# Output-projection weights rounded behind the latest attention work on ScalarE and GpSimd, and the second layer's modulation behind the last softmax denominators

## The chip, the core and the metric

The kernel runs on one core of a Trainium2 chip. The core has a matrix engine (PE, whose weight loads are listed apart as PEld), a vector engine (DVE), a scalar engine (ACT), GpSimd (POOL), and SyncE (SP), from whose queue all transfers here are issued. Each engine works through its own list of instructions in order. The metric is the time of one execution in microseconds (us), the median of several runs.

## What is computed

The reference is a two-layer diffusion backbone in float32 over 2048 latent and 256 context tokens of width 1024. Layer 0 has two attention mixers side by side, a windowed one (8 heads) and a latent-compressed one ("mixer B", 8 heads of 64, over all 2304 keys). Layer 1 has neighbourhood attention (16 heads). Each layer ends in a gated output projection; scale, shift and gate of the next layer come from the conditioning vectors.

```
# mixer B (layer 0): every latent query reads all keys
s = (einsum('bqhd,bkhd->bhqk', qn, kn) + einsum('bqhr,bkr->bhqk', qr, kr)) * scale
p = softmax(s);  ob = einsum('bhqk,bkhd->bqhd', p, v)
# output projection of layer 0, gated
y = concatenate([oa * silu(za), ob * silu(zb)]) @ out_w
# modulation of a layer: one linear map of silu(c), of silu(c_ctx) for context rows
mod = silu(c) @ ada_w + ada_b
```

## The kernel before

Stages run in this order: in0 (input projection), attn_a (windowed attention), out_open(0), attn_b (mixer B), outp(0) (output projection of layer 0), in1, out_open(1), attn_c (neighbourhood attention), outp(1). Most products are three PE matmuls on a rounded high part and a remainder: high x high, low x high, high x low. A matrix that comes from HBM is therefore *split* first: `wsplit` lets ACT copy the loaded tile ws into a rounded tile wh (L260) and POOL subtract it from ws to give the remainder wl (L261). For the output-projection weights these tiles are called wso, who and wlo.

A scheduler lays out the instructions of each engine. It may move an instruction ahead of others that were written before it, where its model of the program lets it start earlier; in attn_b only PE's order is the written one. `tc.issue_after(x)` forbids it to place the instructions inside ahead of instruction x on x's engine.

**attn_b** goes through 8 heads of 2304 queries, in units of 512 queries: t0 = 0, 512, 1024, 1536 and one short unit of 256 for the context. A unit has 18 key tiles. For each tile PE makes three score matmuls (L977 to L979) into one of three PSUM buffers `bs`, ACT takes the exponential twice, rounded into `bph` (L982) and full in place (L983), DVE makes the remainder `bpl` (L984), POOL adds `bph` to the running row sum `bacc` (L988), and four tiles later PE multiplies both parts with the values (`bo`, L997 and L998). `bph` and `bpl` have 8 buffers each. The next tile's L977 into a `bs` buffer needs the L984 that last read it. Between these PE computes the row maxima of the next unit (`bm`, L941, reduced by DVE, L943). At the end of a unit ACT, DVE and POOL take the output out (L1002 to L1007) and PE transposes the row sum (`bdt`, L1015), from which DVE (L1017) makes the denominators.

The weights of the output projection are prepared during the attention. `out_weights_apart` returns, for each of 7 row blocks k of 128 (in layer 1: 3), a step load(k), two transfers on SP, and a step split(k), two `who` on ACT and two `wlo` on POOL. The load buffers wst hold 3 tiles. attn_b runs one such step at units 512 and 1536 of each head from the second: load(k) in the first of them, split(k) in the second. Both stand under an issue_after on the head's value transfer. The eighth block is split by outp itself. attn_c runs them from its 17th item on, at every second one.

**outp(0)**: for each of 8 row blocks the gated input G is made from transfers `o` or `oo` (output), `oz` (gate) and `ord` (one over the denominators, by way of the HBM array s_rd): DVE L1144 to L1146, ACT L1148, POOL L1149 (Gg, Gkh, Gkl). PE makes `y` (L1183). The last denominators of attn_b go through `den_piece`: DVE L675 reciprocal, PE L677 transpose `dnb`, DVE L679 copy `dnsb`, SP L680 store to s_rd. From its third work item on, outp(0) runs four steps (OSIDE) of `mod_rows` for each item, the modulation of layer 1: transfers scb (L190) and adat (L198), ACT L191, and DVE products `mj` (L200).

Of the kernel before, what the change touches and what calls it, by code (L numbers as in the profile page):

```python
# [100 lines left out]
class Kern:  # L101
# [570 lines left out]
    def den_piece(self, p, pt, den, n, dst, nm, tag="pt"):  # L672

        nc = self.nc
        nc.vector.reciprocal(den[:, :n], den[:, :n])  # L675
        ps = pt.tile([P, 512], F32, tag=tag, name=f"dn{nm}")
        nc.tensor.transpose(ps[:n, 0:P], den[:, :n], self.ident)  # L677
        s = p.tile([P, P], F32, tag="dns", bufs=2, name=f"dns{nm}")
        nc.vector.tensor_copy(s[:n, :], ps[:n, 0:P])  # L679
        nc.sync.dma_start(dst.rearrange("(t q) -> t q", q=P), s[:n, :])  # L680
# [169 lines left out]
    def out_weights_apart(self, l, k0, k1, rings):  # L850

        st = {}

        def load(k):
            st[k] = [self.wload(self.wop, self.i[f"wo{l}"][k * P : (k + 1) * P, hf * 512 : (hf + 1) * 512],
                                512, f"o{l}{k}{hf}") for hf in range(2)]

        def split(k):
            self.W.append([self.wsplit(rings, s, 512, f"o{l}{k}{hf}") for hf, s in enumerate(st.pop(k))])
        return [x for k in range(k0, k1) for x in (lambda k=k: load(k), lambda k=k: split(k))]  # L860

    def attn_b(self):
# [5 lines left out]
        with ExitStack() as ctx:  # L868
# [96 lines left out]
            def st_pieces(h, t0, n):  # L965
                t = H[h]
                c = t0 // P
                kts = list(range(NT)) if t0 < TL else [NTL, NTL + 1]
                st = {}

                def score(j):
                    kt = kts[j]
                    if j == 0:
                        st["acc"] = p1.tile([P, 512], F32, tag="acc", bufs=3, name=f"bacc{h}_{c}")
                    ps = sp.tile([P, 512], F32, tag="s", name=f"bs{h}_{c}_{j}")
                    ks, qs = slice(kt * P, (kt + 1) * P), slice(t0, t0 + n)
                    nc.tensor.matmul(ps[:, :n], t["kh"][0:97, ks], t["qh"][0:97, qs], start=True, stop=False)  # L977
                    nc.tensor.matmul(ps[:, :n], t["kh"][0:96, ks], t["ql"][0:96, qs], start=False, stop=False)  # L978
                    nc.tensor.matmul(ps[:, :n], t["kl"][0:96, ks], t["qh"][0:96, qs], start=False, stop=True)  # L979
                    hi = ph.tile([P, 512], R32, name=f"bph{h}_{c}_{j}")  # L980
                    lo = pl_.tile([P, 512], R32, name=f"bpl{h}_{c}_{j}")
                    nc.scalar.activation(hi[:, :n], ps[:, :n], AF.Exp)  # L982
                    nc.scalar.activation(ps[:, :n], ps[:, :n], AF.Exp)  # L983
                    nc.vector.tensor_sub(lo[:, :n], ps[:, :n], f(hi[:, :n]))  # L984
                    if j == 0:
                        st["h0"] = hi
                    else:
                        nc.gpsimd.tensor_add(st["acc"][:, :n], f((st["h0"] if j == 1 else st["acc"])[:, :n]), f(hi[:, :n]))  # L988
                    st[j] = (hi, lo)

                def pv(j):
                    if j == 0:
                        st["o"] = op.tile([P, 512], F32, tag="o", name=f"bo{h}_{c}")
                        st["o2"] = op.tile([P, 512], F32, tag="o2", name=f"bo2{h}_{c}")
                    hi, lo = st.pop(j)
                    fi, la = j == 0, j == len(kts) - 1
                    nc.tensor.matmul(st["o"][:, :n], t["v"][:, kts[j], 0:P], hi[:, :n], start=fi, stop=la)  # L997
                    nc.tensor.matmul(st["o2"][0:65, :n], t["v"][:, kts[j], 64 : P + 1], lo[:, :n], start=fi, stop=la)  # L998

                def fin():  # L1000
                    o = p.tile([P, 512], F32, tag="os", name=f"bos{h}_{c}")
                    nc.scalar.activation(o[:, :n], st["o"][:, :n], AF.Copy)  # L1002
                    o2 = p.tile([65, 512], F32, tag="os2", name=f"bos2{h}_{c}")
                    nc.vector.tensor_copy(o2[:, :n], st["o2"][0:65, :n])
                    acc = st["acc"]
                    nc.gpsimd.tensor_add(o[0:64, :n], o2[0:64, :n], o[0:64, :n])
                    nc.gpsimd.tensor_add(acc[64:65, :n], o2[64:65, :n], acc[64:65, :n])  # L1007
                    for e in range(2):
                        nc.sync.dma_start(scr["o0"][e, 512 + h * 64 : 576 + h * 64, t0 : t0 + n], o[e * 64 : e * 64 + 64, :n])

                def den():
                    d, c0 = den_of(h, t0)
                    ps = xp.tile([P, 512], F32, tag="x", name=f"bdt{h}_{c}")
                    for x in range(n // P):
                        nc.tensor.transpose(ps[:, x * P : (x + 1) * P], st["acc"][:, x * P : (x + 1) * P], self.ident)  # L1015
                    col = t0 // P - c0
                    nc.vector.tensor_reduce(d[:, col : col + n // P], ps[:, :n].rearrange("p (t k) -> p t k", k=P), AX.X, ALU.add)  # L1017
                    late.put(8, lambda: den_done(h, t0, n))

                k = range(len(kts))  # L1020
                return [lambda j=j: score(j) for j in k], [lambda j=j: pv(j) for j in k], fin, den
# [53 lines left out]
    def outp(self, l):  # L1075
        nc, tc, i, scr = self.nc, self.tc, self.i, self.scr
        with ExitStack() as ctx:
# [108 lines left out]
            for n, (c, tt) in enumerate(work):  # L1186
                if tt == 0 and c + 1 < len(chunks):
                    gs = gsteps(c + 1)
                if n + 2 < len(work):
                    c2, t2 = work[n + 2]  # L1190
                    X[(c2, t2)] = res(chunks[c2][0] + t2 * P, c2, t2)
                a = chunks[c][0] + tt * P
                if n < 3:

                    if n == 0:
                        Y = [ytile(x) for x in range(3)]
                        for k in range(KB):
                            for x in range(3):
                                product(Y[x], 0, x, k)
                    ps = Y[n]  # L1200
                else:
                    ps = ytile(n)
                    for k in range(KB):
                        product(ps, c, tt, k)
                x = X[(c, tt)]
                gv = gate[:, 1 if a >= TL else 0, :]
                y = p.tile([P, D], F32, tag="ry", bufs=2, name=f"ry{l}{n}")
                nc.vector.tensor_tensor(y, ps, gv, ALU.mult)
                nc.vector.tensor_add(y, y, x)
                if l == 0:  # L1210
                    lt.put(1, lambda a=a, y=y: nc.sync.dma_start(scr["h1"][a : a + P, :], y))
                else:
                    junk = p.tile([P, D], BF16, tag="oj", bufs=1, name=f"oj{n}")
                    ss = p.tile([P, 1], F32, tag="oss", bufs=3, name=f"oss{n}")
                    nc.scalar.activation(junk, y, AF.Square, accum_out=ss)
                    r = self.rstd(p, ss, D, "o")
                    nc.vector.scalar_tensor_tensor(y, y, r, fg, ALU.mult, ALU.mult)
                    lt.put(1, lambda a=a, y=y: nc.sync.dma_start(self.out[a : a + P, :], y))
                lt.tick()
                for _ in range(OSIDE):  # L1220
                    if side and n > 1:
                        side.pop(0)()
                left = max(1, chunks[c][1] // P - 1 - tt)
                for _ in range(-(-len(gs) // left)):
                    if gs:
                        gs.pop(0)()
# [144 lines left out]
    def attn_c(self):  # L1371
# [5 lines left out]
        with ExitStack() as ctx:  # L1377
# [63 lines left out]
            def make_bias(h, cb):  # L1441
                if cb == 2:
                    return
                b = bias[nbias[0] % 2]
                nbias[0] += 1
                bu = H[h][3]

                for rt, u0, w, d0 in ((0, 128, 384, 128), (1, 0, 512, 0), (2, 0, 384, 128)):
                    nc.gpsimd.tensor_add(b[:, rt, d0 : d0 + w], bu[:, CT[cb], u0 : u0 + w], rm[:, rt, 512 - w : 512])  # L1449
                cur[(h, CT[cb])] = b  # L1450

            def s_pieces(h, cb):
# [7 lines left out]
                def go(rg):  # L1460
# [18 lines left out]
                        op0=ALU.add, op1=ALU.min, accum_out=nm)  # L1479
                    d, c0 = den_of(h, cb)  # L1480
                    col = cb * 4 + rg - c0
                    nc.scalar.activation(s[:, :n], s[:, :n], AF.Exp, bias=nm, scale=-1.0,  # L1482
                                         accum_out=d[:, col : col + 1])
                    Pt[rg] = s
                return [lambda rg=rg: go(rg) for rg in range(4)], Pt

# [193 lines left out]
```

## Time and profile before

| | |
|---|---|
| median of 3 runs | 3673.56 us (3673.25 to 3679.89) |
| the profiled execution | 3666.66 us, of which the span of its instructions is 3664.8 us |
| granted TensorE clock, mean | 0.978 |
| attn_b | about 962 to 1915 us of the span |
| outp(0) | to about 2143 us |
| in1 | to about 2877 us |
| attn_c | about 2877 to 3460 us |

The trace is one execution on the chip. Times in the rows are microseconds from the start of the span. "PE bs L977 <- DVE bpl L984" means that PE stood still before its instruction of line 977 until DVE's of line 984 had ended. PEclk is the share of TensorE's full clock that was granted: 1.00 is the higher of its two levels (2.4 GHz), 0.50 the lower one (1.2 GHz).

### The profile page before, as it was taken

What the parts mean: (1) busy time and instruction counts of PE and PEld (TensorE: products, weight loads), DVE (VectorE), ACT (ScalarE), POOL (GpSimd) and SP (SyncE); (2) the same over time, 40 slices, a digit from 0 to 9 for tenths busy, and PEclk for the clock granted to TensorE, in tenths of its full rate; (3) what the DMA queues carried; (4) which work ended last, traced back from release to release, by engine and by line L of the source; (5) the groups of instructions that cost most, each with busy time, mean ns of one, the idle gap of its engine ahead of it and who ended that gap; (6) DMA issues with size and microseconds to landing.
All of it is one profiled execution on the core that took longest, in us unless ns stands there. A gap on an engine that the chain in (4) does not pass through costs nothing. (4 is left out here: it accounts for less than half of the span.)

```text
span 3664.8 us, 52981 instructions
## 1 busy us (share of the span) xinstructions
PE 3474.2 (95%) x17607; PEld 2871.1 (78%) x17607; DVE 2293.3 (63%) x4313; ACT 1904.1 (52%) x3808; POOL 1759.3 (48%) x1655
## 2 busy tenths in 40 slices
PE   6999989999999999998999999999999999999888
PEld 5787778899877777776767878888888799999766
DVE  6445542399988888987988872213111088888565
ACT  4344333399777777766761142223221288888511
POOL 6555553211488888988893252224122143333432
PEclk8999999999999999999999999999999999999999
DMA  6768564763320222123039955554445476666685
GB/s 218 219 199 261 171 184 128 227 173 83 82 60 18 68 68 68 24 54 80 23 115 302 292 183 168 167 144 127 130 140 146 158 287 238 233 228 231 192 234 172
DMA packets 381051, 576.76 MB, mean 157 GB/s; under 512 B 35393, under 2 KB 218081, under 8 KB 370913
## 3 DMA queue, kind: packets, MB, share of 16 engines
q1 hardware_dynamic: 380777, 573.39, 51.3%
q8 instruction: 138, 2.26, 0.3%
q14 instruction: 136, 1.11, 0.1%
HBM read 399.36 MB, written 173.90 MB: 156 GB/s over the span
## 5 line engine op out<-in xcount | busy, mean ns | idle before, releaser
L261 POOL TENSOR_TENSOR wl<-ws,wh 128x512 fp32r<-128x512 f32 (+2 forms) x320 | 427.1, 1351 | 642.6 <-ACT wh L260 579.2
L988 POOL TENSOR_TENSOR bacc<-bacc,bph 128x512 f32<-128x512 f32 (+1 forms) x528 | 667.5, 1267 | 33.5 <-ACT bph L982 1.8
L982 ACT ACTIVATE bph<-bs 128x512 fp32r<-128x512 f32 (+1 forms) x610 | 353.3, 579 | 215.2 <-PE bs L979 188.8
L943 DVE TENSOR_REDUCE bmx<-bm 128x1 f32<-128x512 f32 (+1 forms) x656 | 406.6, 628 | 67.5 <-PE bm L941 51.5
L984 DVE TENSOR_TENSOR bpl<-bs,bph 128x512 fp32r<-128x512 f32 (+1 forms) x610 | 401.3, 659 | 59.4 <-ACT bs L983 58.1
L983 ACT ACTIVATE bs<-bs 128x512 f32<-128x512 f32 (+1 forms) x610 | 350.7, 575 | 0.0
L260 ACT ACTIVATE wh<-ws 128x512 fp32r<-128x512 f32 (+2 forms) x328 | 197.1, 613 | 266.6 <-DMA ws<-in_w_dram 211.2
L267 PE MATMUL mm<-Uh,wh 128*128 128x512 f32 (+1 forms) x832 | 325.2, 391 | 0.0
L268 PE MATMUL mm<-Ul,wh 128*128 128x512 f32 (+1 forms) x832 | 323.8, 389 | 0.0
L269 PE MATMUL mm<-Uh,wl 128*128 128x512 f32 (+1 forms) x832 | 322.0, 390 | 0.4 <-DVE wl L261 0.4
L1449 POOL TENSOR_TENSOR cbias<-cbu,rm 128x384 f32<-128x384 f32 x144 | 158.3, 1113 | 333.9 <-DVE cnm L1477 194.4
L1477 DVE CUSTOM_DVE_ANT_0 cp<-cs,cbias 128x640 f32<-128x640 f32 (+1 forms) x256 | 222.3, 886 | 135.7 <-PE cs L1473 91.1
L977 PE MATMUL bs<-bqh,bkh 97*128 97x512 f32 (+1 forms) x610 | 246.6, 404 | 42.9 <-DVE bpl L984 42.2
L997 PE MATMUL bo<-bph,bv 128*128 128x512 f32 (+1 forms) x610 | 242.3, 397 | 15.4 <-ACT bos L1002 15.2
L941 PE MATMUL bm<-bkh,bqh 96*128 96x512 f32 (+1 forms) x656 | 244.3, 387 | 4.5 <-DVE bmx L943 3.6
L240 DVE TENSOR_TENSOR plc<-ptc,phc 128x512 fp32r<-128x512 f32 (+1 forms) x384 | 235.3, 640 | 18.1 <-ACT phc L239 17.3
L978 PE MATMUL bs<-bql,bkh 96*128 96x512 f32 (+1 forms) x610 | 240.7, 395 | 0.0
L979 PE MATMUL bs<-bqh,bkl 96*128 96x512 f32 (+1 forms) x610 | 239.0, 392 | 0.0
L998 PE MATMUL bo<-bpl,bv 128*65 128x512 f32 (+1 forms) x610 | 238.0, 390 | 0.4 <-DVE bpl L984 0.2
L200 DVE SCALAR_TENSOR_TENSOR mj<-adat,scb 128x512 bf16<-128x512 f32 x144 | 121.9, 847 | 185.7 <-DMA adat<-in_adat_dram 165.6
L1482 ACT ACTIVATE cp<-cp,cnm 128x640 f32<-128x640 f32 (+1 forms) x256 | 226.3, 884 | 17.6 <-DVE cnm L1477 17.4
L239 ACT ACTIVATE phc<-ptc 128x512 fp32r<-128x512 f32 (+1 forms) x384 | 205.4, 560 | 55.1 <-PE ptc L647 50.8
(314 smaller groups left out, 8870.6 us busy)
## 6 DMA issues: line engine op xcount, KB each, us to landing
ws<-in_w_dram SPq DMA_DIRECT2D x256, 256.0 KB
ck<-s_kcT SPq DMA_DIRECT2D x32, 1152.0 KB
cv<-s_vc SPq DMA_DIRECT2D x64, 512.0 KB
adat<-in_adat_dram SPq DMA_DIRECT2D x96, 256.0 KB
o<-s_o SPq DMA_DIRECT2D x40, 512.0 KB
s_z<-zs SPq DMA_DIRECT2D x64, 256.0 KB
s_qcT<-st SPq DMA_DIRECT2D x64, 256.0 KB
s_kcT<-st SPq DMA_DIRECT2D x32, 512.0 KB
```

The source lines that it names most:

```text
L261: (eng or nc.gpsimd).tensor_sub(l[:, :w], s[:, :w], f(h[:, :w]))
L267: nc.tensor.matmul(out, a[0], b[0], start=first, stop=False)
L268: nc.tensor.matmul(out, a[0], b[1], start=False, stop=False)
L269: nc.tensor.matmul(out, a[1], b[0], start=False, stop=last)
L941: nc.tensor.matmul(ps[:, :w], t["qh"][0:96, b * P : (b + 1) * P], t["kh"][0:96, k0 : k0 + w], start=True, stop=True)
L943: nc.vector.tensor_reduce(t["mx"][:, j : j + 1], ps[:, :w], AX.X, ALU.max)
L977: nc.tensor.matmul(ps[:, :n], t["kh"][0:97, ks], t["qh"][0:97, qs], start=True, stop=False)
L982: nc.scalar.activation(hi[:, :n], ps[:, :n], AF.Exp)
L983: nc.scalar.activation(ps[:, :n], ps[:, :n], AF.Exp)
L984: nc.vector.tensor_sub(lo[:, :n], ps[:, :n], f(hi[:, :n]))
L988: nc.gpsimd.tensor_add(st["acc"][:, :n], f((st["h0"] if j == 1 else st["acc"])[:, :n]), f(hi[:, :n]))
L997: nc.tensor.matmul(st["o"][:, :n], t["v"][:, kts[j], 0:P], hi[:, :n], start=fi, stop=la)
```

## The change

The attention now keeps its latest instruction in two fields: `self.acts` on ACT (the full exponential of a tile in attn_b, of a row group in attn_c) and `self.pools` on POOL (an addition to the row sum in attn_b, of the bias in attn_c). split(k) stands under issue_after of both. `den_piece` keeps its reciprocal in `self.recip`, and the modulation's steps in outp(0) stand under issue_after of that. No instruction is added or removed.

```diff
     def den_piece(...):
-        nc.vector.reciprocal(den[:, :n], den[:, :n])
+        self.recip = nc.vector.reciprocal(den[:, :n], den[:, :n]).ins
...
         def split(k):
-            self.W.append([self.wsplit(...) for hf, s in enumerate(st.pop(k))])
+            with self.tc.issue_after(self.acts), self.tc.issue_after(self.pools):
+                self.W.append([self.wsplit(...) for hf, s in enumerate(st.pop(k))])
...
     def attn_b(self):
-                    nc.scalar.activation(ps[:, :n], ps[:, :n], AF.Exp)
+                    self.acts = nc.scalar.activation(ps[:, :n], ps[:, :n], AF.Exp).ins
...
-                        nc.gpsimd.tensor_add(st["acc"]...)
+                        self.pools = nc.gpsimd.tensor_add(st["acc"]...).ins
...
     def outp(self, l):
                 for _ in range(OSIDE):
                     if side and n > 1:
-                        side.pop(0)()
+                        with tc.issue_after(self.recip):
+                            side.pop(0)()
...
     def attn_c(self):
-                    nc.gpsimd.tensor_add(b[:, rt, d0 : d0 + w], ...)
+                    self.pools = nc.gpsimd.tensor_add(b[:, rt, d0 : d0 + w], ...).ins
...
-                    nc.scalar.activation(s[:, :n], s[:, :n], AF.Exp, bias=nm, ...)
+                    self.acts = nc.scalar.activation(s[:, :n], s[:, :n], AF.Exp, bias=nm, ...).ins
```

The lines of the changed kernel stand one to five further down than those of the kernel before. In names such as bph1_8_17 the numbers are head, first query tile of the unit, and key tile; the last number only tells instances apart.

ACT in head 1, around the first split. Before, it stands behind tile 8 of the head's first unit:

```order
L982 ACTIVATE bph1_0_8_12314<-bs1_0_8_12310 128x512
L983 ACTIVATE bs1_0_8_12310<-bs1_0_8_12310 128x512
L260 ACTIVATE who000_13123<-wso000_12503 128x512
L260 ACTIVATE who001_13127<-wso001_12505 128x512
L982 ACTIVATE bph1_0_9_12336<-bs1_0_9_12332 128x512
L983 ACTIVATE bs1_0_9_12332<-bs1_0_9_12332 128x512
```

and now:

```order
L984 ACTIVATE bph1_8_17_13111<-bs1_8_17_13107 128x512
L985 ACTIVATE bs1_8_17_13107<-bs1_8_17_13107 128x512
L260 ACTIVATE who000_13123<-wso000_12503 128x512
L260 ACTIVATE who001_13127<-wso001_12505 128x512
L984 ACTIVATE bph1_12_0_13136<-bs1_12_0_13132 128x512
L985 ACTIVATE bs1_12_0_13132<-bs1_12_0_13132 128x512
```

The pair has moved from tile 8 of unit 0 to the start of unit 1536, 95 rows further on; heads 2 to 6 show the same.

POOL in head 7, in its last long unit (tile 12 on), while the first G (Gkl) of outp(0) is already being made. Before:

```order
L1006 TENSOR_TENSOR bos7_8_21015<-bos27_8_21017,bos7_8_21015 64x512
L988 TENSOR_TENSOR bacc7_8_20670<-bacc7_8_20670,bph7_8_17_20945 128x512
L988 TENSOR_TENSOR bacc7_12_20961<-bacc7_12_20961,bph7_12_3_21007 128x512
L1149 TENSOR_TENSOR Gkl00_21267<-o005_21330,Gql00_21265 128x512
L1007 TENSOR_TENSOR bacc7_8_20670<-bos27_8_21017,bacc7_8_20670 1x512
L988 TENSOR_TENSOR bacc7_12_20961<-bacc7_12_20961,bph7_12_4_21027 128x512
```

and now:

```order
L990 TENSOR_TENSOR bacc7_12_20961<-bacc7_12_20961,bph7_12_3_21007 128x512
L990 TENSOR_TENSOR bacc7_8_20670<-bacc7_8_20670,bph7_8_17_20945 128x512
L261 TENSOR_TENSOR wlo060_20954<-wso060_20353,who060_20953 128x512
L261 TENSOR_TENSOR wlo061_20958<-wso061_20355,who061_20957 128x512
L990 TENSOR_TENSOR bacc7_12_20961<-bacc7_12_20961,bph7_12_4_21027 128x512
L1010 TENSOR_TENSOR bacc7_8_20670<-bos27_8_21017,bacc7_8_20670 1x512
L1152 TENSOR_TENSOR Gkl00_21267<-o005_21330,Gql00_21265 128x512
```

The seventh split, which stood in head 6, is now here, and the Gkl of row block 5 has four more instructions ahead of it.

DVE at the start of outp(0), around the last denominators (denb). Before:

```order
L1146 TENSOR_TENSOR oo012_21543<-oo012_21543,oz012_21544 128x512
L200 SCALAR_TENSOR_TENSOR mj1_000_21610,mcol0_21607<-adat1_0_0_21608,scb0_21603 128x512
L200 SCALAR_TENSOR_TENSOR mj1_010_21612,mcol0_21607<-adat1_0_0_21608,scb0_21603 128x512
L200 SCALAR_TENSOR_TENSOR mj1_100_21616,mcol0_21607<-adat1_1_0_21614,scb0_21603 128x512
L200 SCALAR_TENSOR_TENSOR mj1_110_21618,mcol0_21607<-adat1_1_0_21614,scb0_21603 128x512
L1017 TENSOR_REDUCE denb7_1536_21222<-bdt7_12_21223 128x4
```

and now:

```order
L1149 TENSOR_TENSOR oo012_21543<-oo012_21543,oz012_21544 128x512
L1020 TENSOR_REDUCE denb7_1536_21222<-bdt7_12_21223 128x4
L675 RECIPROCAL denb7_1536_21222<-denb7_1536_21222 128x4
L200 SCALAR_TENSOR_TENSOR mj1_000_21610,mcol0_21607<-adat1_0_0_21608,scb0_21603 128x512
L200 SCALAR_TENSOR_TENSOR mj1_010_21612,mcol0_21607<-adat1_0_0_21608,scb0_21603 128x512
```

The denominators' reduction and reciprocal have passed the modulation's products.

## Rows read from the trace of the kernel before

**Rows 1.** The page's first part: busy time, share, instructions of each engine.

```profile
PE 3474.2 (95%) x17607; PEld 2871.1 (78%) x17607; DVE 2293.3 (63%) x4313; ACT 1904.1 (52%) x3808; POOL 1759.3 (48%) x1655
```

**Rows 2.** PE's waits, 950 to 1970 us: total us, times, longest us.

```profile
PE bs L977 <- DVE bpl L984: 42.2, 14, 6.9
PE bo L997 <- ACT bos L1002: 15.2, 38, 0.8
PE dnb L677 <- DVE denb L675: 8.3, 1, 8.3
```

**Rows 3.** Waits of the other engines in the same stretch.

```profile
ACT who L260 <- DMA wso<-in_wo_dram: 43.3, 6, 8.1
POOL wlo L261 <- ACT who L260: 37.7, 5, 9.4
ACT bph L982 <- POOL bacc L988: 19.8, 30, 2.6
```

**Rows 4.** SP's order of time, head 1: start, us, queue, line, transfer, count.

```profile
1086.81 9.88 SPq L254 DMA_DIRECT2D wso<-in_wo_dram  x2
```

**Rows 5.** ACT's order of time there; in brackets the idle time before.

```profile
1093.49 0.59 ACT L983 ACTIVATE bs<-bs 128x512 f32<-128x512 f32 x1
1102.18 1.29 ACT L260 ACTIVATE who<-wso 128x512 fp32r<-128x512 f32 x2 [8.10 <-DMA wso<-in_wo_dram]
```

**Rows 6.** PE's order of time there.

```profile
1105.23 0.79 PE L977 MATMUL bs<-bqh,bkh 97*128 97x512 f32 x1 [6.91 <-DVE bpl L984]
```

**Rows 7.** Stretches: length, busy us (count) of PE, PEld, DVE, ACT, POOL, then PEclk.

```profile
1105.20:1109.40 4.20, 4.17 (x10) 3.20 (x11) 3.90 (x7) 2.34 (x5) 3.96 (x4) 0.50 0.00 0
1109.40:1113.60 4.20, 4.20 (x22) 3.35 (x21) 2.81 (x7) 3.63 (x7) 3.96 (x4) 0.99 0.00 0
```

**Rows 8.** Stretches, tile 9 of unit 0 to unit 512: six heads (first, last, sum), head 7.

```profile
1093.80:1116.00 22.20, 15.29 (x62) 11.53 (x62) 12.23 (x24) 10.94 (x21) 13.98 (x12) 0.85 0.39 101
...
1685.90:1708.70 22.80, 16.51 (x63) 12.53 (x63) 12.16 (x24) 11.96 (x23) 15.15 (x13) 0.78 0.55 146
...
sum 131.80, PE 95.83 PEld 72.39 DVE 73.23 ACT 67.02 POOL 85.12; mean PE 15.97 PEld 12.06 DVE 12.21 ACT 11.17 POOL 14.19
...
1810.90:1824.20 13.30, 13.30 (x64) 10.32 (x63) 12.32 (x25) 10.07 (x19) 12.52 (x11) 1.00 0.00 1
```

**Rows 9.** Stretches, unit 512 of head 5 and of head 6.

```profile
1589.30:1616.10 26.80, 26.44 (x119) 20.34 (x118) 24.37 (x45) 20.29 (x39) 23.30 (x19) 1.00 0.05 11
1708.70:1741.20 32.50, 29.75 (x120) 22.02 (x119) 25.04 (x45) 20.63 (x39) 28.43 (x23) 0.89 0.04 9
```

**Rows 10.** Stretch of head 1 without a stall, to the next head's split.

```profile
1109.40:1217.00 107.60, 105.62 (x481) 81.28 (x479) 96.01 (x179) 79.73 (x150) 94.39 (x76) 1.00 0.23 50
```

**Rows 11.** ACT in head 6, unit 512: the longest wait for a bph buffer.

```profile
1720.70 0.60 ACT L982 ACTIVATE bph<-bs 128x512 fp32r<-128x512 f32 x1 [2.64 <-POOL bacc L988]
```

**Rows 12.** The tile wso's instructions on POOL, ns min/median/max: attn_b and outp(0), then outp(0) alone.

```profile
L261 POOL TENSOR_TENSOR wlo<-wso,who x16: 1261/1266/1704, 1102.9 to 1949.9; 128x512 fp32r<-128x512 f32 x16
...
L261 POOL TENSOR_TENSOR wlo<-wso,who x2: 1597/1650/1704, 1938.9 to 1949.9; 128x512 fp32r<-128x512 f32 x2
```

**Rows 13.** DVE's order of time at the start of outp(0).

```profile
1936.80 0.98 DVE L200 SCALAR_TENSOR_TENSOR mj<-adat,scb 128x512 bf16<-128x512 f32 x1 [3.45 <-DMA adat<-in_adat_dram]
...
1941.78 0.68 DVE L1017 TENSOR_REDUCE denb<-bdt 128x4 f32<-128x512 f32 x1
```

**Rows 14.** Stretches at the start of outp(0), columns as in Rows 7.

```profile
1943.30:1949.10 5.80, 5.80 (x15) 4.56 (x16) 3.30 (x9) 0.00 (x0) 0.00 (x0) 0.50 0.96 300
1949.10:1955.00 5.90, 5.90 (x27) 4.74 (x26) 5.90 (x11) 1.26 (x2) 3.20 (x2) 1.00 0.91 301
```

**Rows 15.** POOL's order of time in head 7's last long unit.

```profile
1899.68 1.27 POOL L1007 TENSOR_TENSOR bacc<-bos,bacc 1x512 f32<-1x512 f32 x1
...
1929.13 1.61 POOL L1007 TENSOR_TENSOR bacc<-bos,bacc 1x512 f32<-1x512 f32 x1
```

**Rows 16.** The stretch of attn_c, columns as in Rows 7.

```profile
2877.00:3460.00 583.00, 570.76 (x3962) 522.72 (x3961) 457.10 (x948) 459.22 (x987) 193.15 (x171) 0.99 0.67 231
```

More of the change, by code (lines that the diff above doesn't have):

```diff
@@ L858, in split @@
         def split(k):
-            self.W.append([self.wsplit(rings, s, 512, f"o{l}{k}{hf}") for hf, s in enumerate(st.pop(k))])
+            with self.tc.issue_after(self.acts), self.tc.issue_after(self.pools):
+                self.W.append([self.wsplit(rings, s, 512, f"o{l}{k}{hf}") for hf, s in enumerate(st.pop(k))])
         return [x for k in range(k0, k1) for x in (lambda k=k: load(k), lambda k=k: split(k))]
@@ L987, in score @@
                     else:
-                        nc.gpsimd.tensor_add(st["acc"][:, :n], f((st["h0"] if j == 1 else st["acc"])[:, :n]), f(hi[:, :n]))
+                        self.pools = nc.gpsimd.tensor_add(
+                            st["acc"][:, :n], f((st["h0"] if j == 1 else st["acc"])[:, :n]), f(hi[:, :n])).ins
                     st[j] = (hi, lo)
@@ L1448, in make_bias @@
                 for rt, u0, w, d0 in ((0, 128, 384, 128), (1, 0, 512, 0), (2, 0, 384, 128)):
-                    nc.gpsimd.tensor_add(b[:, rt, d0 : d0 + w], bu[:, CT[cb], u0 : u0 + w], rm[:, rt, 512 - w : 512])
+                    self.pools = nc.gpsimd.tensor_add(
+                        b[:, rt, d0 : d0 + w], bu[:, CT[cb], u0 : u0 + w], rm[:, rt, 512 - w : 512]).ins
                 cur[(h, CT[cb])] = b
@@ L1481, in go @@
                     col = cb * 4 + rg - c0
-                    nc.scalar.activation(s[:, :n], s[:, :n], AF.Exp, bias=nm, scale=-1.0,
-                                         accum_out=d[:, col : col + 1])
+                    self.acts = nc.scalar.activation(s[:, :n], s[:, :n], AF.Exp, bias=nm, scale=-1.0,
+                                                     accum_out=d[:, col : col + 1]).ins
                     Pt[rg] = s
```

## The prediction

> **What bounds the kernel now.** I began with the busy shares: PE works 95% of the span, no other engine comes near [rows 1]. So time is to be had only where PE stands still or runs at the lower clock, and the mean granted clock of 0.978 says that it does. Next I took PE's waits in the stretch of attn_b and the start of outp(0). The reader is to see one large row there: 42.2 us before L977, the first score matmul, in 14 waits, for DVE's L984, the longest 6.9 us [rows 2]. L984 frees the score buffer; but DVE is not slow, since what it waits for is late. The other engines' waits name the cause: ACT stood 43.3 us, six times, before `who` L260, the first half of a split, until its weight tile wso had landed from HBM, and POOL 37.7 us behind it [rows 3].
>
> The order of time in head 1 shows the chain. SP's transfer of wso takes 9.88 us to issue from 1086.81 [rows 4], so the tile lands about 1102. ACT has its list in order, and `who` stands ahead of the exponentials of tile 9: ACT ends a tile at 1094.08 and starts the split at 1102.18, 8.10 us idle [rows 5]. No exponential, no L984, no free buffer: PE restarts at 1105.23 after 6.91 us [rows 6]. Then it runs at the lower clock: 10 matmuls in 4.20 us at 0.50, and in the next 4.20 us 22 at 0.99 [rows 7]. Stall and clock are one loss, and I price them together.
>
> **Six splits that wait, removed.** The stretch from tile 9 of unit 0 to unit 512 holds the same PE work in each head. In the six heads with such a split it takes 131.80 us together; in head 7, which has none, 13.30 at full clock [rows 8]. 131.80 - 6 x 13.30 = 52.0 us. In the new order the pair stands behind the exponentials of tile 17 of unit 1024, 95 ACT rows on, and a tile has two of these: some 46 tiles of 26.80/18 = 1.5 us [rows 9], so over 60 us after the data landed. ACT then has nothing to wait for. **-52.0.**
>
> **The seventh split** stood in head 6 behind the sixth. Its unit 512 takes 32.50 us, the same unit of head 5 26.80 [rows 9]: 5.7 us more. What is late there is not a transfer but POOL, which has two splits on top of a stall to make up: ACT waits up to 2.64 us for a bph buffer that POOL has not yet read [rows 11]. **-5.7.**
>
> **What the splits cost in their new place.** ACT gives 1.29 us to a pair [rows 5], POOL 2 x 1.27 [rows 12]. Over a stretch without a stall ACT is busy 79.73 of 107.60 us and POOL 94.39, both without a split [rows 10], so both have room on average, but the exponentials behind the pair come 1.29 us late at once. Bounds: 0, if the three score buffers cover it, and 1.29 us, if PE feels all of it. The trace shows no split without a wait in the middle of a unit, so neither end is nearer; I take the middle, 0.65, seven times. **+4.5** (0 to 9.0).
>
> **The denominators.** PE stands 8.3 us before `dnb` [rows 2]. DVE's order of time tells why: four `mj` stand ahead of the reduction L1017, the first waited 3.45 us for adat until 1936.80, and the reduction starts at 1941.78 [rows 13]. Behind the gap PE runs 15 matmuls in 5.80 us at 0.50, and 27 in 5.90 at 1.00 [rows 14]; at the latter pace 15 take 3.3, so 2.5 more are lost. With the reduction and the reciprocal ahead of the products, this wait goes: **-10.8.** The products of mj start some 6 us later, and their transfers adat with them on SP. Outp(0) has 200 us to run and nothing in it reads them; in1 does. I cost that at 0, which the rest of outp(0) hides; the price without that cover is those 6 us.
>
> **What is late next there.** The seventh split now lies in head 7's last long unit. On POOL the Gkl of row block 5 gets both `wlo` (2.53 us), one more `bacc` (1.27) and the row L1007 (1.27, [rows 15]) ahead of it: 5.1 us. This Gkl frees the single buffer of the next block's transfers, and DVE's L1144 of that block stands between the L984 of the last unit. The row sum is late by the same chain: POOL's last addition starts at 1929.13 and takes 1.61 [rows 15], PE's transpose `bdt` of it came at once behind, and in the new order `bdt` stands seven matmuls earlier. Bounds: 0, if POOL makes up for it in its waits, and 10.2, if PE feels the delay both in L977 and in `bdt`. I take it once. **+5.1.**
>
> By the rows, `wlo` takes 1.27 us in attn_b, and 1.60 and 1.70 in outp(0), while DVE works on mj, whose two inputs both lie in SBUF [rows 12]. The Trainium skill (GPSIMD Engine Reference, Key points) says that GpSimd shares its SBUF interfaces with VectorE and that instructions of VectorE with two SBUF inputs contend with it. The trace agrees. By this rule the seventh pair, now among DVE's L1144 to L1146, would take up to 3.4 us instead of 2.5, an estimate; the sum would rise by 0.9 us.
>
> **Attn_c.** Three splits move back there too. PE is busy 570.76 of its 583 us [rows 16], no wait of the size seen in attn_b is among what is left, and I cost the move at 0, give or take 1.
>
> **The sum.** -52.0 - 5.7 + 4.5 - 10.8 + 5.1 = **-58.9 us.** The profiled execution would go from 3666.66 to 3607.8. It lies 6.9 us below the median of the runs, 3673.56, so I put the same difference on the median: **3614.7 us**. With the bounds of the two unknown costs (-9.6 and +9.6) it is 3605 to 3624.
>
> **Rivals.**
> *POOL becomes the bound.* POOL loses the idle time of 37.7 us in which it could not work anyway, but a head then takes some 110 us, and POOL needs 94.39 + 2.5 of each 107.6 [rows 10]. Waits for its buffers exist already: 19.8 us in 30 times [rows 3], and the seventh split's loss was wholly of this kind [rows 11]. Against it: they are 0.7 us in the mean, and outside of the stalls the clock stays at 1.00. If every new split cost what the seventh did, 7 x 5.7 = 40 us would come in the place of the 4.5: 3650 us.
>
> *The clock falls at small waits.* PE has 38 waits of up to 0.8 us at the units' ends [rows 2], and the splits add some. In 107.6 us that hold several of them the clock stayed at 1.00 [rows 10]. If it fell behind each split nonetheless, a stretch as in [rows 7] loses 4.2 x 12/22 = 2.3 us, and one as in [rows 14] 2.5: 7 x 2.4 = 17 us, 3632. The Trainium skill (TensorE: Matmul & The Clock Gate, A second HAM failure mode) describes a kernel in which frequent short idle times between groups of matmuls made the clock swing between its two levels; this trace shows none of that, so the chance is small.
>
> *The end of attn_b costs more than outp(0) gains.* If the late row sum brings back the gap before `dnb` with its clock, the 10.8 us stay lost: about 3625.
>
> *The change doesn't do what it says*: the transfer of wso is itself late, and ACT waits at the new place. That needs 60 us of delay on SP; only the 10.8 us would be left, 3663.
>
> *Slower.* In attn_c two wso transfers on SP now stand ahead of the next head's keys ck and queries cq, and wait for a buffer that POOL's `wlo` frees, now behind the bias. If POOL is late, SP holds up the whole next head. One of attn_c's 64 items takes 583/64 = 9.1 us [rows 16]; to eat the 59 us and 7 more, three splits would have to stop PE for 22 us each, over two items. At four items each (109 us) it would be 3724. Against it: POOL is busy for 193 of 583 us [rows 16].
>
> **How the numbers follow.** My forecast 0.75 (3605 to 3624); POOL the bound 0.09 (3625 to 3655); the end of attn_b 0.07 (3625); the clock 0.04 (3632); no effect on the splits 0.02; slower 0.03. The range is to hold 8 in 10: it reaches over the end of attn_b and the clock, **3602 to 3636**. A measurement of this kernel can tell about 0.2% (7 us) from no change. Faster by more: 0.95; within: 0.02; slower: 0.03.
>
> **What would show it.** Right: no wait of ACT for wso in attn_b; PE's wait for L984 down from 42 us to under 10; a clock of 1.00 through the stretches of [rows 8], each near 13.3 us; `dnb` without a gap, or one of a few us before `bdt`; a mean clock above 0.98. Wrong: waits of ACT for POOL's `bacc` well above 19.8 us; a new row "ACT who <- DMA wso"; PE waiting in attn_c for ck or cq; the gap before `dnb` merely moved to `bdt` or to G's products.

## The result, and the profile after

The changed kernel takes 3618.45 us in the median of 4 runs (3611.3 to 3623.49), the kernel before 3673.4 us (3669.39 to 3679.89): ratio 0.9851, 95% interval 0.983 to 0.9872, so 1.5% or 55 us faster. The forecast was 3614.7 us in a range of 3602 to 3636. The profiled execution took 3611.3 us with a span of 3609.5 us; before, the span was 3664.8. The two traces differ by 55.3 us, and most of what follows asks where these lie.

The busy shares of the page hardly move, PE from 95% to 96% (compare [rows 1]):

```profile
PE 3450.7 (96%) x17607; PEld 2853.3 (79%) x17607; DVE 2302.3 (64%) x4313; ACT 1904.8 (53%) x3808; POOL 1765.0 (49%) x1655
```

PE's waits in the stretch of [rows 2], 950 to 1970 us, of the changed kernel (total us, times, longest us):

```profile
PE bo L1000 <- ACT bos L1005: 15.8, 39, 0.8
PE bs L979 <- DVE bpl L986: 11.6, 5, 4.7
PE y L1186 <- DVE dnsb L679: 4.1, 1, 4.1
```

and a row of ACT's, in the stretch of [rows 3]:

```profile
ACT bph L984 <- POOL bacc L990: 21.4, 37, 1.4
```

The 42.2 us before the first score matmul have become 11.6 (its line is now 979), the short waits at the units' ends are what they were, the wait before `dnb` is gone, and a new one stands behind it. No row is left in which ACT waits for wso. ACT's waits for POOL's `bacc` are 21.4 us, where they were 19.8, the longest now 1.4 us. In the stretch of [rows 8], tile 9 of unit 0 to unit 512, the windows of six heads of the changed kernel now read (length; busy us and count of PE, PEld, DVE, ACT, POOL; PEclk):

```profile
1095.30:1108.60 13.30, 13.30 (x63) 10.37 (x63) 12.28 (x24) 10.09 (x19) 12.52 (x11) 1.00 0.65 172
...
1645.90:1659.20 13.30, 13.30 (x63) 10.36 (x63) 12.26 (x24) 9.86 (x19) 12.52 (x11) 1.00 0.70 187
sum 79.80, PE 79.80 PEld 62.12 DVE 73.67 ACT 60.13 POOL 75.10; mean PE 13.30 PEld 10.35 DVE 12.28 ACT 10.02 POOL 12.52
```

All six take 13.30 us, the time of head 7 before, without a gap and at full clock: 52.0 us less. From the first tile of head 1 to that of head 7 it is 660.3 us against 717.0 before.

Head 7 itself went the other way. Its windows, after five others, in the changed kernel:

```profile
1191.40:1741.90 550.50, 540.22 (x2447) 415.44 (x2446) 502.74 (x931) 424.34 (x801) 511.08 (x411) 1.00 0.26 60
```

```profile
1741.90:1865.80 123.90, 106.52 (x439) 77.21 (x438) 104.64 (x173) 84.68 (x160) 112.80 (x85) 0.95 0.25 72
```

The first row is five heads, 110.1 us each; the second, head 7 up to its last score tile, 123.90 us. Before it was 114.0 (1797.1 to 1911.1 in its order of time). Two of PE's waits there are new:

```profile
1849.47 0.79 PE L979 MATMUL bs<-bqh,bkh 97*128 97x512 f32 x1 [4.70 <-DVE bpl L986]
...
1861.39 0.79 PE L979 MATMUL bs<-bqh,bkh 97*128 97x512 f32 x1 [3.83 <-DVE bpl L986]
```

DVE's order of time beside them, in the changed kernel, shows what stood ahead of these `bpl`:

```profile
1843.46 5.36 DVE L1147 TENSOR_TENSOR o<-o 128x512 f32<-128x512 f32 x1 [0.71 <-DMA o<-s_o]
...
1858.19 0.69 DVE L1147 TENSOR_TENSOR o<-o 128x512 f32<-128x512 f32 x1 [2.69 <-DMA o<-s_o]
1860.05 0.69 DVE L1148 TENSOR_TENSOR o<-o 128x512 f32<-128x512 f32 x1 [1.16 <-DMA o<-s_rd]
```

Ahead of the first wait the transfer had come, but an addition that takes 0.69 us elsewhere took 5.36. The second wait ends as in the prediction: POOL's Gkl is late, so the next block's transfer is late, so DVE's list is held. POOL's order of time at that place:

```profile
1842.07 2.54 POOL L990 TENSOR_TENSOR bacc<-bacc,bph 128x512 f32<-128x512 f32 x2
1844.57 2.47 POOL L261 TENSOR_TENSOR wlo<-wso,who 128x512 fp32r<-128x512 f32 x2
1847.01 1.25 POOL L990 TENSOR_TENSOR bacc<-bacc,bph 128x512 f32<-128x512 f32 x1
1848.34 1.60 POOL L1010 TENSOR_TENSOR bacc<-bos,bacc 1x512 f32<-1x512 f32 x1
...
1852.97 1.30 POOL L1152 TENSOR_TENSOR Gkl<-o,Gql 128x512 fp32r<-128x512 f32 x1 [3.02 <-issue]
```

From 1842.07 to 1848.26 POOL works without a pause, each instruction starting a little before the end of the last. The DVE addition, which reads two operands from SBUF as POOL's do, ends at 1848.82, half a microsecond after POOL's first pause. A later section returns to that. POOL was through with the four instructions of the prediction at 1849.94, and then stood still for 3.02 us before the Gkl: its input Gql came from ACT at 1852.84, since DVE's product for it (L1149) could start only behind the addition that was held. So in this trace both waits go back to that addition.

At the start of outp(0), where [rows 13] stood, DVE's order of time in the changed kernel is now:

```profile
1885.96 0.68 DVE L1020 TENSOR_REDUCE denb<-bdt 128x4 f32<-128x512 f32 x1
1886.68 0.18 DVE L675 RECIPROCAL denb<-denb 128x4 f32<-128x4 f32 x1
1889.50 0.69 DVE L200 SCALAR_TENSOR_TENSOR mj<-adat,scb 128x512 bf16<-128x512 f32 x1 [2.65 <-DMA adat<-in_adat_dram]
...
1894.82 0.27 DVE L679 COPY dnsb<-dnb 4x128 f32<-4x128 f32 x1
```

and PE's:

```profile
1889.33 0.27 PE L677 MATMUL dnb<-ident,denb 128*4 128x128 f32 x1
...
1895.14 1.22 PE L1186 MATMUL y<-who,Gqh 128*128 128x512 f32 x2 [4.14 <-DVE dnsb L679]
```

The reciprocal has passed the modulation, and `dnb` starts without a gap. But the copy that empties dnb's PSUM tile has not: four `mj` and the first G product of the next chunk stand between, and the next y needs that tile's place. PE stands 4.14 us there instead of 8.35, and again runs at the lower clock behind it:

```profile
1895.10:1900.90 5.80, 5.76 (x14) 4.55 (x15) 5.50 (x11) 1.78 (x3) 2.24 (x2) 0.52 0.91 287
```

### The profile page after: what moved, and what is told of

Same layout as the page of the kernel before. It is cut to its first block, busy times and chain, and to the rows that moved or that the text cites. A ratio compares the mean times of both kernels' runs of the same rounds, so it can differ in the third digit from the quotient of the medians.

```text
span 3609.5 us, 52993 instructions
## 1 busy us (share of the span) xinstructions
PE 3450.7 (96%) x17607; PEld 2853.3 (79%) x17607; DVE 2302.3 (64%) x4313; ACT 1904.8 (53%) x3808; POOL 1765.0 (49%) x1655
## 4 chain that ended last, share of the span: by engine, by line
PE 67%; DMA 14%; DVE 6%; issue 5%; POOL 4%; ACT 3%; SPq 1%; DVEq 0%; POOLq 0%; ACTq 0%
PE mm L269 7%; PE mm L268 7%; PE mm L267 7%; PE co L656 4%; DMA adat<-in_adat_dram 4%; PE bo L1000 3%; PE ptc L647 3%; PE bm L943 3%; PE bs L979 3%; PE bs L980 3%; PE bo L1001 3%; PE bs L981 3%; DMA o<-s_o 2%; PE ao L656 2%; PE pta L647 2%
## 5 line engine op out<-in xcount | busy, mean ns | idle before, releaser
L979 PE MATMUL bs<-bqh,bkh 97*128 97x512 f32 (+1 forms) x610 | 242.7, 398 | 12.2 <-DVE bpl L986 11.6
```

## The experiments

The stages ahead of attn_b, where nothing was changed, take 962 us in the first two traces and 967 to 973 in all later ones. So runs are compared from the first score matmul on. The table gives the difference of each profiled execution to the trace of the kernel before, in us. The stages are bounded by PE: attn_b ends with the first score matmul of its last tile, outp(0) and in1 with the first score matmul of attn_c, attn_c with the first `y` of outp(1). The stages behind attn_b differ by up to 3 us between three executions of one and the same kernel, the changed one; differences of that size there are not read.

| | attn_b | outp(0), in1 | attn_c | outp(1) | sum | median of the runs |
|---|---|---|---|---|---|---|
| changed kernel, first trace | -45.5 | -9.6 | -1.3 | +0.8 | -55.6 | 3618.45 |
| e5, the same again | -45.2 | -6.7 | -0.2 | +1.5 | -50.6 | 3621.02 |
| e9, the same again | -47.4 | -7.0 | -1.2 | -1.1 | -56.6 | 3620.08 |
| e1, splits only | -44.7 | -4.5 | -0.9 | -1.6 | -51.7 | 3619.54 |
| e2, modulation only | +1.6 | -5.7 | +0.3 | +0.1 | -3.7 | 3672.96 |
| e3, behind the copy | -44.6 | -6.6 | 0.0 | +2.6 | -48.5 | 3625.26 |
| e4, from the first head | -53.2 | +6.9 | +0.2 | +4.4 | -41.7 | 3635.64 |
| e6, three units | -54.8 | -6.0 | +0.2 | +2.7 | -58.0 | 3616.66 |
| e10, the same again | -52.3 | -3.1 | -1.1 | +4.2 | -52.3 | 3615.16 |
| e11, copy on ACT | -52.7 | -7.3 | +8.5 | +2.6 | -48.9 | 3623.92 |
| e7, POOL +2.5 us | -22.9 | -3.2 | +0.8 | +0.3 | -25.0 | 3649.38 |
| e12, POOL +1.3 us | -40.6 | -7.6 | +0.9 | +3.8 | -43.5 | 3635.14 |
| e8, mid-unit | -47.8 | -3.2 | -1.4 | -2.4 | -54.7 | 3620.01 |

The kernel before took 3680.48 us beside e1 to e4, 3679.17 beside e5 to e8, and 3674.08 beside e9 to e12.

### Each part alone (e1, e2)

```diff
# e1: the modulation's steps without the tie
-                        with tc.issue_after(self.recip):
-                            side.pop(0)()
+                        side.pop(0)()
# e2: split(k) without the tie
-            with self.tc.issue_after(self.acts), self.tc.issue_after(self.pools):
-                self.W.append([...])
+            self.W.append([...])
```

> Only the splits are tied, the modulation stands as before. If the two parts of the change are separate, this keeps the six stalls' gain (heads 1 to 6 some 56 us shorter) and head 7's loss of about 10 us, and has again a wait of about 8 us before dnb with the half clock behind it: some 45 to 51 us faster than the kernel before. Rival, that the modulation's tie gains nothing since the wait merely moves to the matmul behind dnb: within 2 us of the changed kernel, so 53 to 57 us faster.

> Only the modulation is tied, the splits stand as before. By the changed kernel's trace the wait before dnb (8.3 us) gives way to one of about 4 us behind it, with the lower clock in both: 3 to 6 us faster than the kernel before. If the splits' place is what lets the modulation's tie work, no difference.

Measured: e1 at 0.9841 of the kernel before (0.9819 to 0.9863), as much as the whole change; e2 at 0.9986 (0.9972 to 0.9999), some 5 us, as expected of it. So the splits carry the gain, and the modulation's tie is worth about 5 us by itself and nothing that these runs resolve on top of the splits. e1 is nearer its rival, 53 to 57 us, than its theory, 45 to 51, but the interval (50 to 67 us) touches both. The waits of e1 show the rival's mechanism in part. PE, 950 to 1960 us:

```profile
PE dnb L677 <- DVE denb L675: 3.6, 1, 3.6
...
PE y L1186 <- DVE dnsb L679: 2.7, 1, 2.7
```

Without the tie the wait before `dnb` is no longer 8.3 us but 3.6, with 2.7 behind it, since in the scheduler's new order one product stands ahead of the reduction, not four; with the tie the whole of it, 4.1, stands behind `dnb`. The list of DVE was moved, and the wait moved along it. (The scheduler's order at in1's start is new too, in e1 as in the changed kernel: PE makes its first transposes of in1's input, `ft`, 16 in a run, where in the kernel before and in e2 it makes 8.)

Head 7 takes 125.7 us in e1, with waits of 2.1 and 5.4 us in L979. But the same addition of DVE takes only 1.78 us there. So head 7 is late by some 10 us without the long hold too.

### Behind the copy instead of the reciprocal (e3), and the copy on ACT (e11)

```diff
# e3
-        self.recip = nc.vector.reciprocal(den[:, :n], den[:, :n]).ins
+        nc.vector.reciprocal(den[:, :n], den[:, :n])
...
-        nc.vector.tensor_copy(s[:n, :], ps[:n, 0:P])
+        self.recip = nc.vector.tensor_copy(s[:n, :], ps[:n, 0:P]).ins
# e11: on the kernel of e6
-        nc.vector.tensor_copy(s[:n, :], ps[:n, 0:P])
+        nc.scalar.activation(s[:n, :], ps[:n, 0:P], AF.Copy)
```

> As the changed kernel, but the modulation is tied behind the copy of the last denominators out of PSUM, not behind their reciprocal. Theory: the 4.1 us of PE before y for the copy, and 2 to 3 us of half clock behind it, are the products that still stand between the reciprocal and the copy; without them no wait is left there and it is 5 to 7 us faster than the changed kernel, about 60 to 62 us faster than before. Rival: the y matmuls then wait for the G products of outp(0), which stand behind the same vector engine: no gain.

> As the one with three steps, but den_piece copies the denominators out of PSUM on ACT, which stands idle there, not on DVE behind the modulation and the G products. Theory: what is left of the waits at the start of outp(0) is DVE's list in order: the wait of y for this copy (1.4 to 4.9 us in the runs so far) goes, with half clock behind it 2 to 5 us faster than the one with three steps. Rival: PE then waits for the reciprocal (dnb) or for the products that free y instead: no gain, or up to 2 us lost to the copies that now lie among the exponentials.

e3's theory fell. DVE's order of time in e3:

```profile
1894.12 0.18 DVE L675 RECIPROCAL denb<-denb 128x4 f32<-128x4 f32 x1
1901.28 0.69 DVE L1147 TENSOR_TENSOR oo<-oo 128x512 f32<-128x512 f32 x1 [6.98 <-DMA oo<-s_o]
1901.89 0.27 DVE L679 COPY dnsb<-dnb 4x128 f32<-4x128 f32 x1
```

No modulation is left ahead of the copy, but one G product is, and that waited 6.98 us for its own transfer. PE stood 4.3 us before y as before. With the copy on ACT (e11) this wait is gone, and PE stands later, for `ry` (DVE's product of y with the gate, which frees the tile of y); of PE's waits in e11, 950 to 1960 us:

```profile
PE y L1186 <- DVE ry L1211: 5.7, 1, 5.7
```

So the rival of both held: something in DVE's list waits for a transfer at this place, and whichever instruction PE needs next stands behind it. PE's waits at this place, `dnb`, its copy and `ry`, are 7.7 us in e6, from which e11 was made, and 6.0 in e11. e11's copies cost more than that: attn_c takes 8.3 and 9.6 us longer than in e6 and e10. A wait of attn_c, in 2870 to 3390 us of e11, for the remainder `plc` that the product with the values (`co`) needs:

```profile
PE co L656 <- DVE plc L240: 9.2, 3, 4.0
```

It is hardly longer than in e6 (8.4) and e10 (7.0). All of PE's waits in this window are 2.6 us longer than in e10; the larger part of the difference is PE's own busy time for the same matmuls, 510.7 us at a mean granted clock of 0.98 against 504.0 at 1.00. That the copies on ACT made these waits, and these the lower clock, is likely and not shown.

### The seventh split out of head 7 (e4, e6, e10)

```diff
# e4: the steps begin in the first head
-                if h > 0 and ch[0][0] in (512, 1536) and side:
+                if ch[0][0] in (512, 1536) and side:
# e6, e10: three units of a head
+                if h > 0 and ch[0][0] in (512, 1024, 1536) and side:
```

> As the changed kernel, but the steps begin in the first head instead of the second, so the seventh split lies in head 6 and none in head 7. Theory: head 7's 9.9 us more (against 114.0 us before) come from the seventh split alone; head 7 is back near 114 us or below and the kernel 8 to 11 us faster than the changed one. Rival: head 7's last unit is late for the G products of outp(0) on DVE and POOL, whatever the split: head 7 stays above 120 us and the gain is under 3 us. The first split's place in head 0 should cost under 1 us by either.

> As the changed kernel, but the steps run at three units of each head from the second on (512, 1024, 1536) instead of two, so all seven splits are done by head 5 and none is left in head 7; in1's order of PE is that of the changed kernel. Theory: the seventh split alone makes head 7's last unit late, by its 5 us on POOL and by the 5.36 us for which one DVE addition is held while POOL works on it: head 7 takes 6 to 10 us less than in the changed kernel, heads 1 to 5 stay at 110 us, and the whole is 5 to 10 us faster than it. Rival: the splits that now lie a head closer, and the transfers that wait for their buffers, cost what head 7 gains: within 3 us of it.

> The kernel with steps at three units of each head, in five rounds. From the first score matmul on its profile was 7.4 us shorter than the changed kernel's on the same chip, 9.6 of it in attn_b: if that holds, 4 to 9 us faster than the changed kernel. If the difference was the spread of the stages behind attn_b, none.

In attn_b all three gain: 53.2, 54.8 and 52.3 us less than before, where the changed kernel has 45.2 to 47.4. Head 7 of e6:

```profile
1752.00:1865.90 113.90, 105.77 (x440) 77.13 (x439) 96.77 (x170) 82.79 (x156) 105.68 (x80) 0.96 0.24 67
```

It takes 113.9 us, what it took before the change, and 11.0 less than in e5 beside it (124.9); in e10 it takes 113.5. In e4 it takes 117.5: one addition of DVE takes 2.92 us there, and PE waits 3.15 us in L979, though head 7 has no split. So the theory held in e6 and e10, and in e4 by some two thirds. In e6 two splits fall in heads 2 and 4, and the heads behind them, 3 and 5, take 2.9 and 0.9 us longer than the others: near their starts PE waits for the last row sum of the head ahead. That heads 1 to 5 stay at 110 us held but for these two.

As a whole, e4 was expected to be 8 to 11 us faster than the changed kernel, and it is some 15 us slower (0.9882 of the kernel before, against 0.9835 in e5; the two did not run side by side). In outp(0) and in1 it loses 6.9 us where the changed kernel gains 6.7 to 9.6: the order of in1 that the scheduler made for e4 is another one, and PE waits at in1's start (1870 to 2950 us of e4) for in1's input `fx` and for its rounded form `Uh`:

```profile
PE ft L345 <- DVE fx L318: 9.9, 2, 6.2
PE mm L267 <- ACT Uh L353: 6.5, 1, 6.5
```

In the changed kernel the first of them is 4.1 us and the second is not there. e6 and e10 keep the changed kernel's order there. Their medians are 4.4 and 4.9 us below those of the changed kernel beside them (0.9827, interval 0.9811 to 0.9844, against 0.9835, 0.982 to 0.985; and 0.9831, 0.9812 to 0.985, against 0.9844, 0.9827 to 0.9861). The intervals overlap, so that the kernel of e6 beats both is likely and not shown; that it has the shorter attn_b is.

### How much room POOL has (e7, e12)

```diff
# e7: both subtractions twice; e12: the first one twice. The second results are read by nobody.
+                if l == 0:
+                    for hf, s in enumerate(ss):          # e12: ss[:1]
+                        x = self.abp.tile([P, 512], BF16, tag="wjk", bufs=2, ...)
+                        self.nc.gpsimd.tensor_sub(x, s, f(self.W[-1][hf][0]))
```

> As the changed kernel, but POOL does the two subtractions of each of attn_b's seven splits twice, the second time into tiles that nobody reads: 2.5 us more of POOL in a head, nothing more on other engines. POOL with room to spare: heads 1 to 6 stay at 110 us, and only head 7's last unit, where DVE is held by POOL's unbroken run, gets longer, by 2 to 5 us. POOL as the bound: each head gets 2.5 us longer or, with the half clock, up to 5, so 15 to 30 us in all.

> As the changed kernel, but POOL does one of the two subtractions of each split of attn_b a second time: 1.27 us more in a head, half of what was added before. There four of seven heads grew from 110 to 114 to 116 us. If POOL's room in a head with a split lies between the two, heads 1 to 6 stay at 110 us; if it was all used up in the changed kernel already, three or four of them get 1.5 to 3 us longer.

Heads 2 to 6 in e12 and, below, in e7 (the changed kernel's row, 550.50 us, stands above):

```profile
1200.40:1755.90 555.50, 541.14 (x2447) 415.21 (x2446) 504.33 (x931) 423.95 (x801) 515.14 (x414) 1.00 0.26 60
```

```profile
1197.00:1763.20 566.20, 547.77 (x2447) 420.12 (x2447) 504.90 (x931) 423.96 (x801) 521.53 (x419) 0.98 0.25 58
```

5 x 1.27 = 6.3 us more on POOL make the five heads 5.0 us longer, 0.5 in the first of them and 1.1 in each of the others; 12.7 us more make them 15.7 longer, 4 to 6 us each in three of them and 0.4 in heads 3 and 6. With attn_b some 23 us longer than in the changed kernel, e7 shows its second case: POOL is the bound. The half dose lands at one place; PE's waits in e12, 1310 to 1756 us, four heads:

```profile
PE bo L1005 <- ACT bos L1010: 8.0, 20, 0.5
PE bdt L1023 <- POOL bacc L1015: 4.4, 4, 1.1
```

Once in each head PE waits 1.1 us for the last addition to the row sum of the unit in which the split lies. In the changed kernel that row doesn't exist in these heads, where the only waits of PE are those for bos. So at this one place POOL has hardly anything to spare for 1.27 us more in front of it, though it is busy for only 511.08 of 550.50 us. This is the room of one place in one order, not of POOL in a head: heads 3 and 6 of e7, where the scheduler let the added subtractions alternate with `wlo`, take twice the load at 0.4 us. e12 lies between its two expectations, nearer the second (three or four heads longer by 1.5 to 3 us), and smaller.

### The split in the middle of a unit (e8)

```diff
-                if h > 0 and ch[0][0] in (512, 1536) and side:
+                if h > 0 and ch[0][0] == 512 and side:
...
                     for j in range(len(score)):
+                        if h > 0 and x[0] == 1024 and j == 9 and side:
+                            with tc.issue_after(self.vdma):
+                                side.pop(0)()
```

> As the changed kernel, but split(k) is run in the middle of a unit, behind tile 8 of unit 1024, instead of at the start of unit 1536. The data has landed there too. If what cost the time was the wait for the transfer alone, heads 1 to 6 stay at 110 us. If the exponentials behind a split are late in the middle of a unit, as the prediction's 0.65 us for each supposes (bounds 0 and 1.29), heads 1 to 6 take 0.5 to 1.3 us longer each.

Measured: five heads in 549.90 us against 550.50:

```profile
1196.10:1746.00 549.90, 539.32 (x2446) 415.99 (x2445) 502.99 (x931) 423.69 (x801) 508.02 (x409) 1.00 0.26 60
```

The exponentials behind a split are 1.29 us late wherever it stands, and PE doesn't feel it. A split in the middle of a unit costs nothing once its data is there, so the wait for the transfer is what cost the time in the old place; this one was in unit 1024, and the old one in unit 0, which no run repeats without the wait. Head 7 takes 123.7 us here, some 10 more than before, though its split lies in unit 1024, well ahead of Gkl.

## Why the prediction was right, and which steps were not

**The six splits: right, to the tenth.** -52.0 us forecast, 131.80 - 79.80 = 52.0 measured, by the same windows. The comparison with head 7, a stretch of the same work without the stall, priced gap and clock together, and e1 shows that the splits alone carry the gain.

**The seventh split's old place: right.** Unit 512 of head 6 takes 26.7 us, as head 5's did; -5.7 forecast, -5.8 measured.

**The new place: too dear.** +4.5 for seven; the six in heads 1 to 6 cost 1.1 us together (52.0 + 5.8 gained at the old places, 56.7 over the six heads). The lower bound of 0 was the right end: the score buffers cover the 1.29 us, at a unit's start and in its middle (e8).

**The end of attn_b: the place right, the size and part of the mechanism not.** The term of +5.1 measured +9.9 us (123.9 against 114.0), near its upper bound of 10.2. The step that failed is that the delay was counted once, as POOL's four instructions ahead of Gkl. It came twice in L979, and in this trace by another way: an addition of DVE was held for 5.36 us, PE waited for it, and by Gql and Gkl it made the next transfer late too. The named links, Gkl, transfer, DVE's list, are the last of the second wait, but POOL itself was ready 3.02 us earlier. The sentence on the Trainium skill pointed at the contention, at the seventh pair among DVE's additions with two SBUF inputs, but sized it by POOL's own duration (+0.9 us; the pair took 2.47 us); here it was DVE that paid. That the split in head 7 causes most of the loss is shown: head 7 takes 123.7 to 125.8 us with it (changed kernel, e5, e1, e8, e12), and 113.9 and 113.5 without (e6, e10), 117.5 in e4. Why it is some 10 us and not 5 is shown for the one trace alone: e1 loses as much without the long hold, and e8 with the split a unit earlier.

**The denominators: the wrong step.** -10.8 us forecast. PE's wait fell from 8.35 to 4.14 us, and the lower clock came back behind it: 14 matmuls in 5.8 us where there were 15 [rows 14]. That is a gain of some 4 us, and e1, without the tie, has waits of 6.3 us there (3.6 and 2.7), so that the tie itself is worth some 2. The step that failed is "with the reduction and the reciprocal ahead of the products, this wait goes". The next instruction of the same chain on DVE, the copy, was not followed: it stayed behind the products in DVE's list, as the order of the changed program shows.

**What was costed at 0.** In outp(0) and in1 the kernel gains 9.6, 6.7 and 7.0 us in three traces, some 3 to 5 more than at the denominators; in1's first transposes wait 4.1 us in the first of them instead of 7.3. The prediction has no term for it, and where it comes from is not shown: these transposes stand in another order now, which neither tie asked for, but e1, which has that order, gains 4.5 us in outp(0) and in1, and e2, which hasn't, 5.7. Attn_c is at 0 within 1.3. No slower rival showed itself.

**The rival of POOL** was given 0.09 with the argument that it had room on average, 96.9 of 107.6 us. The forecast was right there by a narrow margin: e12 adds 1.27 us to a head and pays 1.0 for it. The average said nothing of the one place where POOL's last addition is waited for. **The rival of the clock** is excluded: it stays at 1.00 through five heads with their 25 waits of up to 0.8 us. **The end of attn_b costing the gain of outp(0)**, given 0.07, is right in that 9.9 us were lost there and some 4 won here; its mechanism, a late row sum that brings back the gap before `dnb`, did not occur, and neither did its 3625. Of the signs named, PE's wait for the score buffer is 11.6 us and not under 10, by head 7 alone, and the gap before `dnb` moved in part behind it, one of the signs of being wrong. That the sum came out so near the forecast is in part luck: errors of 4.8 us (the end of attn_b) and 6.6 (the denominators) to the bad met others of 3.4 (the new place) and some 5 (the rest of outp(0) and in1) to the good: -56.7 in heads 1 to 6, +9.9 in head 7, -9.6 to attn_c, +1.0 in all the rest make -55.4, against -58.9.

## What to carry to other kernels

An instruction that waits for a transfer holds everything behind it on its engine, so a step that isn't needed yet belongs behind the latest work that is; its price is read best by comparing the same stretch with and without it, which takes the lower clock in with the gap. When a step is moved, follow each chain it touches to its last instruction: a tie to the reciprocal left the copy behind, and PE waited there instead; a tie to the copy (e3) left it behind a product that waited 6.98 us for its own transfer. And don't take idle time for room: add a known load to the engine and see where it is paid.

## What the runs showed of the hardware

The DVE instructions of `o` and `oo` with two operands in SBUF (0.69 us alone) take longer beside POOL, whose instructions here read two operands in SBUF as well. Most often such an instruction ends 0.55 us after the one POOL instruction beside which it began, and POOL's next one takes longer for it. In the changed kernel, DVE and then POOL:

```profile
1899.05 1.76 DVE L1148 TENSOR_TENSOR oo<-oo,ord 128x512 f32<-128x512 f32 x1
1900.74 1.77 DVE L1147 TENSOR_TENSOR oo<-oo 128x512 f32<-128x512 f32 x1
```

```profile
1898.66 1.61 POOL L1152 TENSOR_TENSOR Gg<-oo,Gg 128x512 fp32r<-128x512 f32 x1 [5.65 <-ACT Gg L1151]
1900.22 3.45 POOL L261 TENSOR_TENSOR wlo<-wso,who 128x512 fp32r<-128x512 f32 x2
```

POOL makes no pause here, Gg ends at 1900.27 and the first `wlo` at about 1901.95, and DVE's two end at 1900.81 and 1902.51; the two `wlo` take 1.7 us each instead of 1.27. Of 34 such DVE instructions that begin beside POOL between 1700 and 2150 us, 30 end so, three end while the same POOL instruction runs on, and one is held over four: the 5.36 us above. In all the traces together 13 are held for 2.9 to 6.1 us over two to five POOL instructions, none of them in e1 and e11. Twelve of the 13 end some half a microsecond after the end of a POOL instruction behind which POOL pauses. The longest, in e7, DVE and then POOL:

```profile
1868.74 6.14 DVE L1152 TENSOR_TENSOR o<-o 128x512 f32<-128x512 f32 x1 [1.21 <-DMA o<-s_o]
```

```profile
1866.91 2.53 POOL L261 TENSOR_TENSOR wlo<-wso,who 128x512 fp32r<-128x512 f32 x2
1869.41 2.47 POOL L866 TENSOR_TENSOR wjk<-wso,who 128x512 bf16<-128x512 f32 x2
1871.85 1.25 POOL L1014 TENSOR_TENSOR bos<-bos,bos 64x512 f32<-64x512 f32 x1
1873.07 1.25 POOL L995 TENSOR_TENSOR bacc<-bacc,bph 128x512 f32<-128x512 f32 x1
1874.40 1.60 POOL L1015 TENSOR_TENSOR bacc<-bos,bacc 1x512 f32<-1x512 f32 x1
```

POOL works from 1866.91 to 1874.32 and pauses; DVE ends at 1874.88. But a pause is not what it takes: the two cases above end without one, and so does one of the 13, in e12, again DVE and then POOL:

```profile
1858.69 5.37 DVE L1152 TENSOR_TENSOR o<-o 128x512 f32<-128x512 f32 x1 [0.76 <-POOL bacc L995]
```

```profile
1862.24 1.25 POOL L866 TENSOR_TENSOR wjk<-wso,who 128x512 bf16<-128x512 f32 x1
1863.46 1.71 POOL L995 TENSOR_TENSOR bacc<-bacc,bph 128x512 f32<-128x512 f32 x1
```

What decides whether DVE waits for one POOL instruction or for several stays open. `bpl`, which reads one operand from PSUM, kept its 0.69 us throughout. The Trainium skill (GPSIMD Engine Reference, Key points) says that GpSimd shares its SBUF interfaces with VectorE and contends with instructions of VectorE that have two SBUF inputs. The traces agree: instructions with two such inputs grew to 1.8 us and in 13 cases to 2.9 and more, and `bpl` did not. That the shared access is the cause is not shown, since no run here varied the operands alone.
